# Linear attention in a two-layer trunk: chunk decays behind the first levels, sample operands of 128 rows, one product for key and query

## The chip, the cores and the metric

The kernel runs on one core of one Trainium2 chip. The metric is device time in microseconds for one launch. Five engines work side by side, each with its own queue of instructions that it takes in order: TensorE (PE, matrix products), VectorE (DVE), ScalarE (ACT, functions such as exp), GpSimd (POOL) and SyncE (SP, which issues transfers). An instruction that needs another engine's result waits on a semaphore, and all that stands behind it on its engine waits too.

## The reference, cut to what matters

Two layers, each with token mixing and a convolutional feed-forward part, over 64 sample tokens (8 sequences of 8) and 512 prompt tokens, model width 1024, all in f32. The mixing has softmax attention (8 heads), HGRN linear attention (4 heads, key 128, value 64) and GLA linear attention (4 heads, key 32, value 64). The change is in the last two, both of which compute:

```
def step(S, inp):                      # chunks of 64 tokens (8 for the samples)
    qc, kc, vc, gc = inp
    b = jnp.cumsum(gc, axis=2)         # summed log forget gates
    inter = einsum('nhtk,nhkv->nhtv', qc * jnp.exp(b), S)
    diff = b[:, :, :, None, :] - b[:, :, None, :, :]
    decay = where(causal, jnp.exp(jnp.minimum(diff, 0.0)), 0.0)
    scores = einsum('nhtk,nhsk,nhtsk->nhts', qc, kc, decay)
    intra = einsum('nhts,nhsv->nhtv', scores, vc)
    b_last = b[:, :, -1:, :]
    S = exp(b_last) * S + einsum('nhsk,nhsv->nhkv', kc * jnp.exp(b_last - b), vc)
    return S, inter + intra
```

## The kernel before

All 576 tokens are kept together, channels on partitions, in two halves of 320 and 256 tokens. An f32 projection is split into three products of rounded parts (lines 125, 126 and 127: weight-high by input-high, weight-low or input-low by the other's high part); one projection of 128 output channels is 24 such matmuls a half. Its weights come by DMA into `wraw`, ScalarE makes the high part `whi` (line 106), VectorE the low part `wlo` (line 107).

`mixing` goes through first projections, `values`, four HGRN heads (`hgrn_head`, j = 0 to 3), one tile with all four GLA heads (j = 4), then attention. Both kinds call `gla_tile`. It computes, with b the summed log gates:

- the diagonal: `own` = q x k (line 447), summed by small products (453, 455);
- six levels B = 1, 2, 4, 8, 16, 32 (`level_tile`): GpSimd takes differences of b within blocks (413, 414), ScalarE their exp (415), VectorE multiplies the early half by k (416) and the late half by q (418); TensorE multiplies the two (471 for the sample tokens, in the first three levels, 477 for the prompt), and VectorE copies the scores under a mask into `sds` and `sd` (439). The tile `lev` has two buffers;
- `qe` = exp(b) x q (483, 488), `al` (485, 486) and `ke` = exp(b_last - b) x k (499, 501, 502), the chunk decays;
- transposes of ke (508, 511), state products U for the prompt (517) and for the samples (531, with `vm` from GpSimd, 529), the running states;
- outputs from scores and states (548 to 557); line 554 is the samples' product of `vs` and `sds`.

`finish` normalises a pair of heads: `rsqrt` on GpSimd (243) gives `rh` and `rhs`, products at 692 to 706 spread them. The same helper gives `rr`, the norm of the inputs, which line 269 broadcasts before a layer's first decays. The sample operands have 64 rows (the 64 sample tokens), the prompt's 128.

The order in which each engine takes its instructions is not the order of the code: a scheduler in the framework simulates the engines and their dependences and moves independent work (projections of later heads above all) in between. Where the code says `with behind(ins)`, an instruction is not issued, in that simulation, before `ins`; the table FILL uses this to place some loads and projections.

```
def behind(ins):
    return tc.issue_after(ins) if ins is not None else nullcontext()
```

Of the kernel before, what the change touches and what calls it, by code (L numbers as in the profile page):

```python
# [8 lines left out]
F32 = mybir.dt.float32  # L9
# [4 lines left out]
ALU = mybir.AluOpType  # L14
# [5 lines left out]
P = 128  # L20
# [52 lines left out]
def trunk_kernel(ctx: ExitStack, tc: tile.TileContext, I, O):  # L73
# [329 lines left out]

    def level_tile(hp, q, k, b, B, t0, qbd):
# [6 lines left out]
        bv, ev, qv, kv = view(b), view(e), view(q), view(k)  # L411
        ref = bv[:, :, 0, B - 1:B].to_broadcast([P, n, B])
        G.tensor_tensor(ev[:, :, 0, :], ref, bv[:, :, 0, :], ALU.subtract)  # L413
        G.tensor_tensor(ev[:, :, 1, :], bv[:, :, 1, :], ref, ALU.subtract)
        S.activation(e[:, t0:T], e[:, t0:T], AF.Exp)
        V.tensor_tensor(ev[:, :, 0, :], ev[:, :, 0, :], kv[:, :, 0, :], ALU.mult)
        if qbd is None:
            V.tensor_tensor(ev[:, :, 1, :], ev[:, :, 1, :], qv[:, :, 1, :], ALU.mult)
        else:
            for h in range(4):  # L420
                r = slice(32 * h, 32 * h + 32)
                V.tensor_tensor(view(qbd[:, h, :])[r, :, 1, :], ev[r, :, 1, :], qv[r, :, 1, :], ALU.mult)
        return e

    def gla_tile(l, hp, q, k, b, heads, kd, vt, vs, vcol, s0, o_ps, os_ps, outs, qbd, j):

# [17 lines left out]
        sds = hp.tile([TS, nh, TS], F32, name="sds", tag=f"sds{nh}", bufs=2 if nh == 1 else 1)  # L444
        sdm = sd.rearrange("p c h t -> p (c h) t")
# [9 lines left out]
        PE.matmul(bp[:TS, 4 * nh:5 * nh], own[:, 0:TS], sums, start=True, stop=True)  # L455
        for dst, rows, c0 in ((sdm, P, 0), (sds, TS, 4 * nh)):
            m = dst.shape[1]
            V.tensor_tensor(dst, dmask[:rows, None, :].to_broadcast([rows, m, 64]),
                            bp[:rows, c0:c0 + m, None].to_broadcast([rows, m, 64]), ALU.mult)
        for lv, B in enumerate((1, 2, 4, 8, 16, 32)):  # L460
            sample = B <= 4
            xk = xq = level_tile(hp, q, k, b, B, 0 if sample else TS, qbd)
            if qbd is not None:
                xq = qbd

            def moving(c0):
                return late(xq[:, c0:c0 + 64] if qbd is None else xq[:, :, c0:c0 + 64], B)

            if sample:
                bs = s_bank()  # L470
                PE.matmul(bs[:TS, :nh * 32], xk[:, 0:TS], moving(0), start=True, stop=True)
                level_scores(B, lv, sds, bs[:TS, :nh * 32])
            bp = s_bank()
            for cp in range(4):
                for hh in range(2):
                    c0 = TS + P * cp + 64 * hh
                    mm = PE.matmul(bp[64 * hh:64 * hh + 64, cp * nh * 32:(cp + 1) * nh * 32],  # L477
                                   xk[:, c0:c0 + 64], moving(c0), start=True, stop=True)
            mark(f"h{j}.{lv}", mm)
            level_scores(B, lv, sdm, bp[:, :128 * nh])  # L480

        qe = hp.tile([P, T], F32, name="qe", tag="qe", bufs=2)
        S.activation(qe, b, AF.Exp)
        al = hp.tile([P, 16], F32, name="al", tag="al", bufs=2)
# [11 lines left out]
        for t0, t1, w in ((0, TS, 8), (TS, T, 64)):  # L496
            bv = b[:, t0:t1].rearrange("p (c t) -> p c t", t=w)
            n = (t1 - t0) // w
            G.tensor_tensor(ke[:, t0:t1].rearrange("p (c t) -> p c t", t=w),
                            bv[:, :, w - 1:w].to_broadcast([P, n, w]), bv, ALU.subtract)  # L500
        S.activation(ke, ke, AF.Exp)
        V.tensor_tensor(ke, ke, k, ALU.mult)

        kT = hp.tile([P, 512], F32, name="kT", tag="kT", bufs=1)
        kTs = hp.tile([TS, P], F32, name="kTs", tag="kTs", bufs=1)
        tb = t_bank()
# [4 lines left out]
        PE.transpose(tb[:TS, :P], ke[:, 0:TS], ident)  # L511
        S.activation(kTs, tb[:TS, :P], AF.Copy)

# [13 lines left out]
        for i, (r0, _, _) in enumerate(heads):  # L527
            vm = hp.tile([TS, NB, 64], F32, name="vm", tag="t512", bufs=2)
            G.tensor_tensor(vm, vs[:TS, None, vcol + i * 64:vcol + (i + 1) * 64].to_broadcast([TS, NB, 64]),
                            bmask[:, :, None].to_broadcast([TS, NB, 64]), ALU.mult)  # L530
            mm = PE.matmul(ub[r0:r0 + kd, :], kTs[:, r0:r0 + kd],
                           vm.rearrange("p b v -> p (b v)"), start=True, stop=True)
# [6 lines left out]
        def head_outputs(i):  # L539
# [5 lines left out]
            for c in range(8):  # L545
# [22 lines left out]
    def mixing(l, act, first):  # L568
# [16 lines left out]
        with ExitStack() as mx:  # L585
# [63 lines left out]
            with ExitStack() as hx:  # L649
                hp = hx.enter_context(tc.tile_pool(name=f"hp{l}", bufs=1, reuse_waits="tile"))  # L650
                vb = [hp.tile([P, 4, 2, 256], F32, name=f"vb{i}") for i in range(2)]
                for t in vb:
                    G.memset(t, 0.0)
                vbs = [hp.tile([P, 256], F32, name=f"vbs{i}") for i in range(2)]
                rt = hp.tile([P, 5, 16], F32, name="rt")
                wg = hp.tile([16, P], F32, name="wg")
                SP.dma_start(wg, I["w_g"][l])

                works = {}
# [58 lines left out]
                def hgrn_head(j):  # L718
# [6 lines left out]
                    V.tensor_tensor_scan(b, scm, f, 0.0, ALU.mult, ALU.add)  # L725
                    return gla_tile(l, hp, q, k, b, [(0, j % 2, j // 2)], P, vb[0], vbs[0], j * 64, s0,
                                    o_ps, os_ps, (O["hp"][l, j], O["hs"][l, j]), None, j)[0]

# [33 lines left out]
                for t0, n in HALVES:  # L762
# [8 lines left out]
                V.tensor_tensor_scan(b, scm, z, 0.0, ALU.mult, ALU.add)  # L771
                outputs = gla_tile(l, hp, q, k, b, [(32 * i, i % 2, 2 + i // 2) for i in range(4)], 32,
                                   vb[1], vbs[1], 0, s0, o_ps, os_ps, (O["gp"][l], O["gs"][l]), qbd, 4)
                for i in range(2):
# [518 lines left out]
```

## Time and profile before

| what | value |
|---|---|
| device time, median of 3 (lowest, highest) | 1745.67 us (1742.08, 1746.49) |
| the profiled execution's own time | 1746.23 us |
| its span in the profile | 1744.4 us |
| TensorE busy | 1685.0 us, 97% |
| VectorE, ScalarE, GpSimd busy | 63%, 43%, 26% |
| granted TensorE clock, mean over the span | 0.986 |

The linear-attention stage runs from about 37 to 262 us in layer 1 and from about 906 to 1130 us in layer 2. In the page and in the trace each instruction stands with its line of the kernel, its engine, and out<-in by the names of the tiles. Idle time in square brackets names what ended it.

### The profile page before, as it was taken

What the parts mean: (1) busy time and instruction counts of PE and PEld (TensorE: products, weight loads), DVE (VectorE), ACT (ScalarE), POOL (GpSimd) and SP (SyncE); (2) the same over time, 40 slices, a digit from 0 to 9 for tenths busy, and PEclk for the clock granted to TensorE, in tenths of its full rate; (3) what the DMA queues carried; (4) which work ended last, traced back from release to release, by engine and by line L of the source; (5) the groups of instructions that cost most, each with busy time, mean ns of one, the idle gap of its engine ahead of it and who ended that gap; (6) DMA issues with size and microseconds to landing.
All of it is one profiled execution on the core that took longest, in us unless ns stands there. A gap on an engine that the chain in (4) does not pass through costs nothing.

```text
span 1744.4 us, 36125 instructions
## 1 busy us (share of the span) xinstructions
PE 1685.0 (97%) x14688; PEld 1588.6 (91%) x14688; DVE 1100.8 (63%) x2220; ACT 747.3 (43%) x1289; POOL 450.8 (26%) x780
## 2 busy tenths in 40 slices
PE   8999999899999999999999999999999999999997
PEld 8888997689899999999998888967899999999997
DVE  6765665665874564666667666566577736647664
ACT  6644424464543332333356534254645333323331
POOL 4543432301610010110264543332044101001103
PEclk9999999999999999999999999999999999999999
DMA  5211236748253635632322212368463446266231
GB/s 180 75 62 57 82 114 238 274 176 300 86 185 115 241 107 190 236 129 88 117 85 87 68 51 89 133 251 316 136 256 136 144 168 217 78 226 254 72 108 55
DMA packets 65670, 260.93 MB, mean 150 GB/s; under 512 B 9664, under 2 KB 18144, under 8 KB 63968
## 3 DMA queue, kind: packets, MB, share of 16 engines
q1 hardware_dynamic: 65504, 258.62, 42.1%
q8 instruction: 116, 1.90, 0.4%
q14 instruction: 50, 0.41, 0.1%
HBM read 245.39 MB, written 80.31 MB: 187 GB/s over the span
## 4 chain that ended last, share of the span: by engine, by line
PE 85%; DVE 4%; ACT 4%; POOL 3%; issue 3%; DMA 1%; SPq 0%; POOLq 0%; ACTq 0%; DVEq 0%
PE ps_m L125 22%; PE ps_m L126 22%; PE ps_m L127 22%; PE ps_s L477 2%; PE ps_o L916 1%; PE ps_o L862 1%; PE ps_s L837 1%; POOL x L345 1%; PE ps_t L853 1%; DVE pi L849 1%; PE ps_m L397 1%; PE ps_m L396 1%; PE ps_m L398 1%; DMA wraw<-in_w_of 1%; PE ps_m L627 1%
## 5 line engine op out<-in xcount | busy, mean ns | idle before, releaser
L106 ACT ACTIVATE whi<-wraw 128x1024 fp32r<-128x1024 f32 (+4 forms) x232 | 222.2, 963 | 316.6 <-PE ps_m L126 230.1
L107 DVE TENSOR_TENSOR wlo<-wraw,whi 128x1024 fp32r<-128x1024 f32 (+4 forms) x232 | 261.2, 1130 | 139.2 <-ACT whi L106 132.9
L125 PE MATMUL ps_m<-xha,whi 128*128 128x320 f32 x1088 | 341.3, 314 | 0.7 <-DVE y L375 0.6
L126 PE MATMUL ps_m<-xla,whi 128*128 128x320 f32 x1088 | 340.1, 313 | 0.0
L127 PE MATMUL ps_m<-xha,wlo 128*128 128x320 f32 x1088 | 339.3, 313 | 0.0
L126 PE MATMUL ps_m<-xlb,whi 128*128 128x256 f32 x1088 | 310.9, 286 | 0.0
L127 PE MATMUL ps_m<-xhb,wlo 128*128 128x256 f32 x1088 | 310.6, 285 | 0.0
L125 PE MATMUL ps_m<-xhb,whi 128*128 128x256 f32 x1088 | 310.3, 285 | 0.2 <-DVE smx L894 0.2
L125 PEld LDWEIGHTS ps_m<-xhb,whi 128*128 128x128 f32 x1088 | 209.0, 192 | 3.9 <-issue 3.4
L127 PEld LDWEIGHTS ps_m<-xhb,wlo 128*128 128x128 f32 x1088 | 209.1, 192 | 1.3 <-issue 0.7
L126 PEld LDWEIGHTS ps_m<-xlb,whi 128*128 128x128 f32 x1088 | 208.9, 192 | 1.0 <-issue 0.2
L125 PEld LDWEIGHTS ps_m<-xha,whi 128*128 128x128 f32 x1088 | 206.9, 190 | 2.6 <-DVE y L375 1.1
L126 PEld LDWEIGHTS ps_m<-xla,whi 128*128 128x128 f32 x1088 | 206.6, 190 | 2.4 <-issue 1.7
L125 PE MATMUL ps_m<-hh,whi 128*128 128x320 f32 (+1 forms) x704 | 208.4, 296 | 0.2 <-DVE y L1061 0.2
L127 PE MATMUL ps_m<-hh,wlo 128*128 128x320 f32 (+1 forms) x704 | 208.3, 296 | 0.0
L126 PE MATMUL ps_m<-hl,whi 128*128 128x320 f32 (+1 forms) x704 | 208.0, 295 | 0.0
L127 PEld LDWEIGHTS ps_m<-xha,wlo 128*128 128x128 f32 x1088 | 205.9, 189 | 2.0 <-issue 1.5
L125 PEld LDWEIGHTS ps_m<-hh,whi 128*128 128x128 f32 x704 | 132.9, 189 | 0.4 <-DVE y L1061 0.4
L126 PEld LDWEIGHTS ps_m<-hl,whi 128*128 128x128 f32 x704 | 133.0, 189 | 0.0
L127 PEld LDWEIGHTS ps_m<-hh,wlo 128*128 128x128 f32 x704 | 132.8, 189 | 0.0
L1002 DVE TENSOR_TENSOR u<-ps_m,rbc 128x256 f32<-128x256 f32 x82 | 34.9, 425 | 115.9 <-PE ps_m L127 115.7
L413 POOL TENSOR_TENSOR lev<-work 128x288 f32<-128x288 f32 (+1 forms) x60 | 49.5, 825 | 157.9 <-DVE work L725 46.4
(305 smaller groups left out, 3254.3 us busy)
## 6 DMA issues: line engine op xcount, KB each, us to landing
wraw<-in_w_up SPq DMA_DIRECT2D x88, 512.0 KB, 3.7
kv<-in_ck SPq DMA_DIRECT2D x32, 768.0 KB, 6.8
kv<-in_cv SPq DMA_DIRECT2D x32, 768.0 KB, 6.7
out_ck<-in_ck SPq DMA_DIRECT2D x32, 768.0 KB, 7.4
out_cv<-in_cv SPq DMA_DIRECT2D x32, 768.0 KB, 6.5
wraw<-in_w_s SPq DMA_DIRECT2D x42, 512.0 KB, 3.5
wraw<-in_w_dn SPq DMA_DIRECT2D x32, 384.0 KB, 3.1
wraw<-in_w_v SPq DMA_DIRECT2D x12, 512.0 KB, 3.4
```

The source lines that it names most:

```text
L106: S.activation(hi[:, :n], raw[:, :n], AF.Copy)
L107: V.tensor_tensor(lo[:, :n], raw[:, :n], hi[:, :n].bitcast(F32), ALU.subtract)
L125: PE.matmul(out, ah, bh, start=(i == 0), stop=False)
L126: PE.matmul(out, ah, bl, start=False, stop=False)
L127: PE.matmul(out, al, bh, start=False, stop=(i == n - 1))
L345: (V if dram_out and k % 4 == 3 else G).tensor_tensor(xk, xk, yk, ALU.add)
L396: PE.matmul(b[:, :n], wh, xh, start=(k == 0), stop=False)
L397: PE.matmul(b[:, :n], wl, xh, start=False, stop=False)
L398: PE.matmul(b[:, :n], wh, xl, start=False, stop=(k == KT - 1))
L413: G.tensor_tensor(ev[:, :, 0, :], ref, bv[:, :, 0, :], ALU.subtract)
L477: mm = PE.matmul(bp[64 * hh:64 * hh + 64, cp * nh * 32:(cp + 1) * nh * 32], xk[:, c0:c0 + 64], moving(c0), start=True, stop=True)
L1002: V.tensor_tensor(u[:, 338:594], b[:, :n], R[:, t0:t0 + n], ALU.mult)
```

## The change

There are three parts. (1) In `gla_tile` the exp of qe is issued behind the second level's exp (`exps[1]`), the subtractions of ke behind the third level's second subtraction (`subs[2]`), and ke's exp behind the third level's exp. (2) `vbs`, `vm`, `sds` and `kTs` become tiles of 128 rows that live for a whole layer; eight GpSimd memsets at the layer's start put zeros into rows 64 to 127 (2048 columns in all), and the sample products at 531 and 554 contract over 128 rows. `vm` leaves the pair of buffers that it shared with `sn` and the squares of `finish`, and has two of its own. (3) For the HGRN heads one VectorE op multiplies the early half by k and the late half by q: the key takes the first slot of the tile `work` and the query the second, and a strided view reads both. The GLA tile keeps its separate products.

```
         G.tensor_tensor(ev[:, :, 0, :], ref, bv[:, :, 0, :], ALU.subtract)
-        G.tensor_tensor(ev[:, :, 1, :], bv[:, :, 1, :], ref, ALU.subtract)
-        S.activation(e[:, t0:T], e[:, t0:T], AF.Exp)
-        V.tensor_tensor(ev[:, :, 0, :], ev[:, :, 0, :], kv[:, :, 0, :], ALU.mult)
+        sub = G.tensor_tensor(ev[:, :, 1, :], bv[:, :, 1, :], ref, ALU.subtract)
+        exp = S.activation(e[:, t0:T], e[:, t0:T], AF.Exp)
         if qbd is None:
-            V.tensor_tensor(ev[:, :, 1, :], ev[:, :, 1, :], qv[:, :, 1, :], ALU.mult)
+            both = kq[:, t0:t0 + 2 * (T + B)].rearrange("p (two r) -> p two r", two=2)[:, :, 0:T - t0]
+            both = both.rearrange("p two (n x) -> p n two x", x=2 * B)[:, :, :, 0:B]
+            V.tensor_tensor(ev, ev, both, ALU.mult)
...
-        S.activation(qe, b, AF.Exp)
+        with behind(exps[1]):
+            S.activation(qe, b, AF.Exp)
...
-            G.tensor_tensor(ke[:, t0:t1].rearrange("p (c t) -> p c t", t=w),
-                            bv[:, :, w - 1:w].to_broadcast([P, n, w]), bv, ALU.subtract)
-        S.activation(ke, ke, AF.Exp)
+            with behind(subs[2]):
+                G.tensor_tensor(ke[:, t0:t1].rearrange("p (c t) -> p c t", t=w),
+                                bv[:, :, w - 1:w].to_broadcast([P, n, w]), bv, ALU.subtract)
+        with behind(exps[2]):
+            S.activation(ke, ke, AF.Exp)
...
-            vm = hp.tile([TS, NB, 64], F32, name="vm", tag="t512", bufs=2)
-            G.tensor_tensor(vm, vs[:TS, None, vcol + i * 64:vcol + (i + 1) * 64].to_broadcast([TS, NB, 64]),
+            vm = vms[(i + j) % 2]
+            G.tensor_tensor(vm[:TS], vs[:TS, None, vcol + i * 64:vcol + (i + 1) * 64].to_broadcast([TS, NB, 64]),
...
-            PE.matmul(os_[rows, :], vs[:TS, cols], sds[:, i, :], start=True, stop=False)
+            PE.matmul(os_[rows, :], vs[:, cols], sds[:, i, :], start=True, stop=False)
...
+                vms = [hp.tile([P, NB, 64], F32, name=f"vm{i}") for i in range(2)]
+                sds1 = [hp.tile([P, 1, TS], F32, name=f"sds{i}") for i in range(2)]
+                sds4 = hp.tile([P, 4, TS], F32, name="sds4")
+                kTs = hp.tile([P, P], F32, name="kTs")
+                for t in (*vbs, *vms, *sds1, sds4, kTs):
+                    G.memset(t[TS:], 0.0)
...
-                        works[j] = [t[:, i, :] for i in range(4)]
+                        kqs[j] = t.rearrange("p i t -> p (i t)")
+                        works[j] = [t[:, i, :] for i in (1, 0, 2, 3)]
```

The scheduler answers the new constraints with another order. On TensorE, head 0 of layer 1, the order was this, from the level-0 sample product (471) on; `ke` is the chunk decay of the keys, `xha` and the like are inputs of head 1's query projection:

```order
L471 MATMUL ps_s<-lev 64x32
L508 MATMUL ps_t<-con,ke 128x128 x4
L511 MATMUL ps_t<-con,ke 64x128
L125 MATMUL ps_m<-xha_141,whi 128x320
L126 MATMUL ps_m<-xla_143,whi 128x320
L125 MATMUL ps_m<-xhb_142,whi 128x256
L126 MATMUL ps_m<-xlb_144,whi 128x256
L477 MATMUL ps_s<-lev 64x32 x8
```

The transposes stood ahead of the projection. Now, at the same place (line 471 has become 480):

```order
L480 MATMUL ps_s<-lev 64x32
L125 MATMUL ps_m<-xha_141,whi 128x320
L126 MATMUL ps_m<-xla_143,whi 128x320
L125 MATMUL ps_m<-xhb_142,whi 128x256
L126 MATMUL ps_m<-xlb_144,whi 128x256
L127 MATMUL ps_m<-xha_141,wlo 128x320
L125 MATMUL ps_m<-xha_145,whi 128x320
```

The projection follows the sample product directly; the prompt's level-0 products come 30 projection matmuls later, the transposes after more than 70.

On ScalarE, same place, before (`vb` and `rt` are evacuations of `values`, `qe` belongs to heads 0 and 1):

```order
L483 ACT_TABLE_LOAD
L483 ACTIVATE qe_776<-work_314 128x576
L483 ACTIVATE qe_1006<-work_315 128x576
L415 ACTIVATE lev_671<-lev_671 128x576
L639 ACTIVATE rt_311<-ps_m_592,rr1_486 128x16
L645 ACTIVATE vb0_305<-ps_m_592,rr1_486 64x256 x2
L501 ACTIVATE ke_782<-ke_782 128x576
L106 ACTIVATE whi_823<-wraw_821 128x1024
```

and now:

```order
L417 ACT_TABLE_LOAD
L417 ACTIVATE lev_684<-lev_684 128x576
L650 ACTIVATE rt_325<-ps_m_606,rr1_500 128x16
L656 ACTIVATE vb0_305<-ps_m_606,rr1_500 64x256 x2
L106 ACTIVATE whi_828<-wraw_826 128x1024
L106 ACTIVATE whi_1049<-wraw_1047 128x1024
```

The level's exp comes first, and neither a qe nor a ke exp stands between it and the split of the weights.

On TensorE at the start of layer 2, the broadcast of `rr` (269) stood here among the first products of `values` (125 to 127 and 627):

```order
L127 MATMUL ps_m<-whi,xla_10040 128x272
L125 MATMUL ps_m<-whi,xha_10042 128x272
L269 MATMUL ps_t<-con,rr_10588 128x128 x2
L627 MATMUL ps_m<-wlo,xha_10042 128x272
L627 MATMUL ps_m<-whi,xha_10046 128x272
```

and now, 20 matmuls further on, here:

```order
L125 MATMUL ps_m<-whi,xha_10026 128x272
L126 MATMUL ps_m<-wlo,xha_10026 128x272
L269 MATMUL ps_t<-con,rr_10574 128x128 x2
L127 MATMUL ps_m<-whi,xla_10028 128x272
```

In layer 1 that broadcast has kept its place.

## Rows read from the trace of the kernel before

**Rows 1.** Page, part 1: each engine's busy us, share, instructions.

```profile
PE 1685.0 (97%) x14688; PEld 1588.6 (91%) x14688; DVE 1100.8 (63%) x2220; ACT 747.3 (43%) x1289; POOL 450.8 (26%) x780
```

**Rows 2.** Table by stretch: stretch and length, busy per engine, clock, DMA.

```profile
37.00:262.00 225.00, 216.83 (x2267) 198.11 (x2265) 150.20 (x290) 107.49 (x161) 95.79 (x110) 0.98 0.24 78
480.00:500.00 20.00, 20.00 (x153) 20.00 (x152) 15.84 (x27) 8.57 (x13) 4.62 (x14) 1.00 0.68 252
```

**Rows 3.** TensorE's waits: us in total, times, longest.

```profile
PE ps_s L471 <- DVE lev L418: 5.5, 2, 2.7
...
PE ps_t L508 <- DVE ke L502: 2.9, 2, 1.5
...
PE ps_s L453 <- DVE own L447: 2.5, 2, 1.3
...
PE ps_s L477 <- DVE lev L418: 2.0, 2, 1.0
...
PE ps_t L700 <- POOL rh L243: 1.4, 2, 0.7
```

**Rows 4.** Timeline, TensorE, head 0 of layer 1: start, us, instruction, wait.

```profile
49.72 0.27 PE L471 MATMUL ps_s<-lev 128*64 128x32 f32 x2 [2.72 <-DVE lev L418]
51.52 1.09 PE L508 MATMUL ps_t<-con,ke 128*128 128x128 f32 x4 [1.53 <-DVE ke L502]
...
52.48 0.62 PE L125 MATMUL ps_m<-xha,whi 128*128 128x320 f32 x1
```

**Rows 5.** Timeline, ScalarE, the same place.

```profile
45.77 1.26 ACT L483 ACTIVATE qe<-work 128x576 f32<-128x576 f32 x2
46.93 0.67 ACT L415 ACTIVATE lev<-lev 128x576 f32<-128x576 f32 x1
...
48.76 0.68 ACT L501 ACTIVATE ke<-ke 128x576 f32<-128x576 f32 x1
...
49.35 1.99 ACT L106 ACTIVATE whi<-wraw 128x1024 fp32r<-128x1024 f32 x2
```

**Rows 6.** Line 447, all instances: duration min/median/max in ns.

```profile
L447 DVE TENSOR_TENSOR own<-work x10: 743/754/1246, 39.6 to 1030.6; 128x576 f32<-128x576 f32 x10
```

**Rows 7.** Page, part 5: busy us, mean ns, idle before (line 107).

```profile
L107 DVE TENSOR_TENSOR wlo<-wraw,whi 128x1024 fp32r<-128x1024 f32 (+4 forms) x232 | 261.2, 1130 | 139.2 <-ACT whi L106 132.9
```

**Rows 8.** Timeline, GpSimd, start of layer 2.

```profile
896.76 3.55 POOL L653 MEMSET vb<- 128x2048 f32 x2
```

**Rows 9.** Timeline, GpSimd, start of layer 1.

```profile
32.02 1.41 POOL L243 TENSOR_TENSOR rr<-rv,mhalf 128x2 f32<-128x2 f32 x1 [1.77 <-DVE rv L242]
```

**Rows 10.** Table by stretch around the stretches of low clock.

```profile
52.00:58.00 6.00, 6.00 (x38) 5.68 (x37) 5.37 (x7) 3.56 (x7) 5.03 (x4) 0.55 0.52 178
922.00:926.00 4.00, 4.00 (x33) 3.71 (x33) 3.37 (x6) 2.71 (x5) 3.95 (x3) 0.70 0.61 200
142.00:147.00 5.00, 5.00 (x39) 4.48 (x39) 4.45 (x10) 1.44 (x3) 2.27 (x2) 0.66 0.29 94
```

**Rows 11.** Timeline, GpSimd, head 2 of layer 1.

```profile
112.66 1.29 POOL L499 TENSOR_TENSOR ke<-work 128x64 f32<-128x64 f32 x2
```

**Rows 12.** Timeline, three engines, head 2 of layer 1.

```profile
104.04 1.06 ACT L106 ACTIVATE whi<-wraw 128x1024 fp32r<-128x1024 f32 x1 [5.38 <-PE ps_m L126]
...
114.19 0.45 DVE L418 TENSOR_TENSOR lev<-lev,work 128x288 f32<-128x288 f32 x1
...
115.76 0.24 PE L471 MATMUL ps_s<-lev 128*64 128x32 f32 x1
```

**Rows 13.** Timeline, TensorE, state products of head 0.

```profile
60.08 1.05 PE L517 MATMUL ps_t<-vb,kT 128*128 128x128 f32 x8
61.06 1.12 PE L531 MATMUL ps_t<-vm,kTs 64*128 64x512 f32 x2
62.12 0.39 PE L125 MATMUL ps_m<-xhb,whi 128*128 128x256 f32 x1
```

**Rows 14.** Line 488, all instances.

```profile
L488 DVE TENSOR_TENSOR qe<-qe,work x8: 1215/1360/1584, 49.5 to 1006.7; 128x576 f32<-128x576 f32 x8
```

More of the change, by code (lines that the diff above doesn't have):

```diff
@@ L401, in first_tiles, with level_tile @@
                 e(b, hf, t0, n)
-    def level_tile(hp, q, k, b, B, t0, qbd):
+    def level_tile(hp, q, kq, b, B, t0, qbd):
         n = (T - t0) // (2 * B)
@@ L409, in view @@
             return t[:, t0:T].rearrange("p (n two w) -> p n two w", two=2, w=B)
-        bv, ev, qv, kv = view(b), view(e), view(q), view(k)
+        bv, ev = view(b), view(e)
         ref = bv[:, :, 0, B - 1:B].to_broadcast([P, n, B])
         G.tensor_tensor(ev[:, :, 0, :], ref, bv[:, :, 0, :], ALU.subtract)
-        G.tensor_tensor(ev[:, :, 1, :], bv[:, :, 1, :], ref, ALU.subtract)
-        S.activation(e[:, t0:T], e[:, t0:T], AF.Exp)
-        V.tensor_tensor(ev[:, :, 0, :], ev[:, :, 0, :], kv[:, :, 0, :], ALU.mult)
+        sub = G.tensor_tensor(ev[:, :, 1, :], bv[:, :, 1, :], ref, ALU.subtract)
+        exp = S.activation(e[:, t0:T], e[:, t0:T], AF.Exp)
         if qbd is None:
-            V.tensor_tensor(ev[:, :, 1, :], ev[:, :, 1, :], qv[:, :, 1, :], ALU.mult)
-        else:
+            both = kq[:, t0:t0 + 2 * (T + B)].rearrange("p (two r) -> p two r", two=2)[:, :, 0:T - t0]
+            both = both.rearrange("p two (n x) -> p n two x", x=2 * B)[:, :, :, 0:B]
+            V.tensor_tensor(ev, ev, both, ALU.mult)
+        else:
+            kv, qv = view(kq[:, 0:T]), view(q)
+            V.tensor_tensor(ev[:, :, 0, :], ev[:, :, 0, :], kv[:, :, 0, :], ALU.mult)
             for h in range(4):
@@ L422, in level_tile, with gla_tile @@
                 V.tensor_tensor(view(qbd[:, h, :])[r, :, 1, :], ev[r, :, 1, :], qv[r, :, 1, :], ALU.mult)
-        return e
-    def gla_tile(l, hp, q, k, b, heads, kd, vt, vs, vcol, s0, o_ps, os_ps, outs, qbd, j):
+        return e, sub.ins, exp.ins
+    def gla_tile(l, hp, kq, q, k, b, heads, kd, vt, vs, vcol, s0, o_ps, os_ps, outs, qbd, j, sds, vms, kTs):
         nh = len(heads)
@@ L443, in gla_tile @@
         sd = hp.tile([P, 4, nh, 64], F32, name="sd", tag=f"sd{nh}", bufs=2 if nh == 1 else 1)
-        sds = hp.tile([TS, nh, TS], F32, name="sds", tag=f"sds{nh}", bufs=2 if nh == 1 else 1)
         sdm = sd.rearrange("p c h t -> p (c h) t")
@@ L455, in gla_tile @@
         PE.matmul(bp[:TS, 4 * nh:5 * nh], own[:, 0:TS], sums, start=True, stop=True)
-        for dst, rows, c0 in ((sdm, P, 0), (sds, TS, 4 * nh)):
+        for dst, rows, c0 in ((sdm, P, 0), (sds[:TS], TS, 4 * nh)):
             m = dst.shape[1]
@@ L459, in gla_tile @@
                             bp[:rows, c0:c0 + m, None].to_broadcast([rows, m, 64]), ALU.mult)
+        subs, exps = [], []
         for lv, B in enumerate((1, 2, 4, 8, 16, 32)):
             sample = B <= 4
-            xk = xq = level_tile(hp, q, k, b, B, 0 if sample else TS, qbd)
+            xk, sub, exp = level_tile(hp, q, kq, b, B, 0 if sample else TS, qbd)
+            xq = xk
+            subs.append(sub)
+            exps.append(exp)
             if qbd is not None:
@@ L471, in gla_tile @@
                 PE.matmul(bs[:TS, :nh * 32], xk[:, 0:TS], moving(0), start=True, stop=True)
-                level_scores(B, lv, sds, bs[:TS, :nh * 32])
+                level_scores(B, lv, sds[:TS], bs[:TS, :nh * 32])
             bp = s_bank()
@@ L498, in gla_tile @@
             n = (t1 - t0) // w
-            G.tensor_tensor(ke[:, t0:t1].rearrange("p (c t) -> p c t", t=w),
-                            bv[:, :, w - 1:w].to_broadcast([P, n, w]), bv, ALU.subtract)
-        S.activation(ke, ke, AF.Exp)
+            with behind(subs[2]):
[3 more added lines that the diff above has]
+            S.activation(ke, ke, AF.Exp)
         V.tensor_tensor(ke, ke, k, ALU.mult)
         kT = hp.tile([P, 512], F32, name="kT", tag="kT", bufs=1)
-        kTs = hp.tile([TS, P], F32, name="kTs", tag="kTs", bufs=1)
         tb = t_bank()
@@ L511, in gla_tile @@
         PE.transpose(tb[:TS, :P], ke[:, 0:TS], ident)
-        S.activation(kTs, tb[:TS, :P], AF.Copy)
+        S.activation(kTs[:TS, :], tb[:TS, :P], AF.Copy)
         ub = t_bank()
@@ L657, in mixing @@
                 SP.dma_start(wg, I["w_g"][l])
-                works = {}
+                works, kqs = {}, {}
                 def work(j):
@@ L725, in hgrn_head @@
                     V.tensor_tensor_scan(b, scm, f, 0.0, ALU.mult, ALU.add)
-                    return gla_tile(l, hp, q, k, b, [(0, j % 2, j // 2)], P, vb[0], vbs[0], j * 64, s0,
-                                    o_ps, os_ps, (O["hp"][l, j], O["hs"][l, j]), None, j)[0]
+                    return gla_tile(l, hp, kqs[j], q, k, b, [(0, j % 2, j // 2)], P, vb[0], vbs[0], j * 64, s0,
+                                    o_ps, os_ps, (O["hp"][l, j], O["hs"][l, j]), None, j, sds1[j % 2], vms, kTs)[0]
                 outputs = []
@@ L771, in mixing @@
                 V.tensor_tensor_scan(b, scm, z, 0.0, ALU.mult, ALU.add)
-                outputs = gla_tile(l, hp, q, k, b, [(32 * i, i % 2, 2 + i // 2) for i in range(4)], 32,
-                                   vb[1], vbs[1], 0, s0, o_ps, os_ps, (O["gp"][l], O["gs"][l]), qbd, 4)
+                outputs = gla_tile(l, hp, kqs[4], q, k, b, [(32 * i, i % 2, 2 + i // 2) for i in range(4)], 32,
+                                   vb[1], vbs[1], 0, s0, o_ps, os_ps, (O["gp"][l], O["gs"][l]), qbd, 4,
+                                   sds4, vms, kTs)
                 for i in range(2):
```

## The prediction

> **What bounds the kernel now.** I read the page's busy line first: TensorE is busy 97% of a span of 1744.4 us, the next engine 63% [rows 1]. So what counts is the time in which TensorE waits, runs at its low clock, or streams something slower than need be. Then the table by stretch: the linear-attention stage of layer 1, 225 us, holds 216.83 us of TensorE work, that is 8.2 us of idling, where 20 us in the middle of the feed-forward part have none [rows 2]. The same table gives the pitch of a projection matmul, 20.00 / 153 = 0.131 us. The waits of TensorE say what those 8.2 us are: level products that wait for the decayed operands (5.5 us in two waits, one in each layer), transposes that wait for ke (2.9), the diagonal sums that wait for `own` (2.5), later level products (2.0), the norm's broadcast that waits for `rh` (1.4) [rows 3]. Every entry is there twice, one wait in each layer. All of these lie on the path, for TensorE has nothing else in front of it then, by its order.
>
> The biggest of them is one place, head 0 (the first linear-attention head). The level-0 sample product starts at 49.72 after 2.72 us of idling, the four transposes of ke at 51.52 after another 1.53, and only at 52.48 the first matmul of head 1's query projection [rows 4]. ScalarE's rows say why: two qe exps stand ahead of the level-0 exp (45.77 for 1.26 us, then 46.93), and the ke exp stands ahead of the weight split (48.76, then whi from 49.35) [rows 5]. So the work that TensorE needs last (transposes, state) is queued ahead of what it needs first.
>
> **Part by part.** *The exps moved.* On ScalarE the level-0 exp takes the place of the qe exps: it runs from 45.77 to 46.44. The product with the key and the query is then one VectorE op; the same shape of op, `own`, takes 0.75 us in the middle [rows 6], so the level-0 sample product can go at 47.3 instead of 49.72. Behind the exp stand the evacuations that filled 47.60 to 48.76 before, 1.16 us [rows 5], then head 1's weight split directly: whi from 47.6 to 48.6 (two took 1.99), and wlo on VectorE, 1.13 us on average [rows 7], until about 49.75. By the new order four projection matmuls need only whi (4 x 0.131 = 0.52 us, done in the gap), the rest follow without a stop. So the projection runs as though it had begun at 49.75 - 0.52 = 49.2. The transposes, which took from 51.52 to 52.48, are now 0.96 us of work further on, and some 0.2 us of small products move with them: 50.4 against 52.48, a gain of 2.1 us. What is late next is wlo, which then leaves about half of the 4.25 us of idling. Bounds: 0 (the fused op and the split both queue behind contended VectorE work) to 4.25.
>
> In layer 2 the same two waits stand (2.7 and 1.4 in the sums of [rows 3]), but something is put ahead: the eight zero fills come before the rsqrt `rr` on GpSimd. Together they have 2048 columns, as one fill of vb, which takes 3.55 / 2 = 1.8 us [rows 8]; that row ends where `rr` began, so `rr` is 1.8 us later, and the order puts its broadcast 20 matmuls later, 20 x 0.131 = 2.6 us. The decays start that much later and would give the gain back, but in layer 2 the new order also puts the whole of head 1's query projection ahead of the level-0 product, and its weights do not wait for `rr`. I take layer 1's 2.1 us here too; bounds are 0 and the whole 4.1, and -2.6 if the projection's split too hangs behind the late evacuations. In layer 1 the fills cost nothing: GpSimd stood idle 1.77 us ahead of `rr` [rows 9], as long as the fills take; without that cover it would be 1.8.
>
> *The clock.* After head 0's gap the granted clock is 0.55 over 52 to 58 us, with TensorE busy all of the 6.00, which costs 0.45 x 6 = 2.7 us; in layer 2 it is 0.70 over 922 to 926, 0.30 x 4 = 1.2 us [rows 10]. That is the lower of the two levels (1.2 GHz) for a part of the time, behind idling of 2.7 and 1.5 us with a few tiny products between. With idling of half the size and a projection in the middle of it I let half go: 3.9 / 2 = 1.95 us. Bounds 0 to 3.9. A second such stretch in layer 1, 142 to 147 at 0.66, costs 0.34 x 5 = 1.7 us [rows 10]; the change spreads the products there among projections differently, and I take half again, 0.85, with bounds -1.7 (it comes up in layer 2 as well) and 1.7.
>
> *The other heads.* Per layer they wait 1.25 for `own`, 1.0 for a level, 0.7 for `rh` [rows 3]. For `rh`: GpSimd ran the two ke subtractions, 1.29 us, ahead of vm and rh [rows 11]; with these behind level 2, rh comes 1.29 us earlier and the 0.7 go. The 1.0 goes too, since qe's and ke's VectorE ops leave from ahead of the level ops. `own` is not touched. Against it a new wait of 0.9 us is to be expected at head 2's level 0: from the weight split at 104.04, which starts when a TensorE projection (head 2's forget gate) has freed its buffers, TensorE needed until 115.76 for that head's level-0 product, 11.7 us, while VectorE was done at 114.64 (114.19 + 0.45), 1.1 us ahead [rows 12]. The new order has 35 projection matmuls in this stretch where 58 stood, 23 x 0.131 = 3.0 us less cover, and 26 small products moved in, at most 1.2 us: 1.8 to 3.0 less against 1.1 of slack, so 0.7 to 1.9; I take 0.9, because rh's own products move behind it. Net 2 x (1.0 + 0.7 - 0.9) = 1.6 us. Bounds -2.4 and 5.9.
>
> *The zero rows.* Eight U products of 128 contraction rows take 61.06 - 60.08 = 0.98 us for 1024 columns; the pair with 64 rows that follows has as many columns and lasts to 62.12, 1.06 us, and the matmul behind it shows 0.39 [rows 13]. With 128 rows I give the pair 0.98, and 0.04 for the weight load behind it, 0.12 us for each of eight HGRN heads: 1.0. Bounds 0 (the delay is the weight load's alone, and stays) and 2.0 (the four-head tile gains too). A loss is excluded by the 128-row products themselves, which are no slower a column.
>
> *Key and query in one op.* Two ops of half the columns take 0.45 us each where nothing disturbs them [rows 12]; one takes 0.75 as `own` does, or 1.22 to 1.58 as the qe product, the same shape, does in its eight instances [rows 14]. So a level gains 0.15 us or loses 0.3 to 0.7. VectorE is not the bound, so it counts only where TensorE waits for a level, five or six times: -4 to +1; I take 0, since head 0's term already has the 0.75. The Trainium skill, "SBUF — State Buffer", section "SBUF: two separate sides", holds that a VectorE op with two operands in SBUF and a GpSimd op that reads SBUF exclude each other for a whole instruction. The spread of the two rows, 0.743 to 1.246 and 1.215 to 1.584, agrees with it, and by it the fused op, which keeps the lock in one piece, would meet GpSimd's subtractions of the next level and cost the upper figure.
>
> **The sum.** 2.1 + 2.1 + 1.95 + 0.85 + 1.6 + 1.0 = 9.6 us. The profiled execution took 1746.23 us; 1746.2 - 9.6 = 1736.6. The median of the runs is 0.56 below the profiled one, so the forecast is 1736 us.
>
> **Rivals.**
> - *Slower.* The chain of head 2 keeps its pace of 10.6 us (104.04 to 114.64) and its fused op takes 1.4 instead of 0.9 beside GpSimd, while TensorE gets there 1.8 to 3.0 earlier. If head 3 and the first broadcast run dry in the same way, each layer has two such waits of about 1.9, and the clock falls behind them as it does behind head 0, 1.2 to 2.7 a layer [rows 10]: 2 x (3.8 + 2.0) = 11.6 lost against 2.1 + 2.1 + 1.0 gained and nothing of the other terms. That is 6.4 slower, 1752. It decides from about 2.6 us of new waiting a layer. For it: 58 became 35. Against it: level 0 no longer waits behind qe and ke there.
> - *No change.* Layer 2's 2.6 us of delay cancels its 2.1, and the clock still falls, since the gap is shorter but not gone; what remains is 2.1 + 1.0 + a little: 3 us, 1743. For it: the gaps in front of both slow stretches stay at about 2 us.
> - *Larger gain.* Neither slow stretch comes back (3.9 + 1.7 instead of 2.8), and the waits of the middle heads go for the most part (4.5 instead of 1.6): 9.6 + 2.8 + 2.9 = 15.3, 1730.
> - *The fills do nothing for TensorE*, the pair keeps its 1.06: 1.0 less, 1737, inside the forecast.
>
> **Chances and range.** The forecast's own case, some 1732 to 1740: 0.42. Larger gain: 0.15. No change to a small gain (1740 to 1747): 0.26. Slower: 0.17. I call within 0.3% (5.2 us of 1745.67, so 1740.4 to 1750.9) no change, which is about what a measurement of this kernel can tell. From the cases: faster 0.42 + 0.15 + 0.04 = 0.61; slower by more than that 0.11; the same 0.28. The range from 1727 to 1750 leaves out about one in ten on each side; the likeliest case alone has 1732 to 1740.
>
> **What would show it.** Right: TensorE's wait for the first level product in each layer falls to about a microsecond, no wait for ke is left in head 0, the projection of head 1 begins before 49 us, the wait for `rh` is gone; the 64-row pair's successor starts 0.1 us sooner; the clock over 52 to 58 is above 0.75. Wrong: a new wait of over 2 us for a level operand or `own` in heads 2 or 3, the clock as low as before, or the fused op at 1.2 us and more in its median with TensorE waiting behind it. In layer 2, a projection that begins only after 920 us would say that the fills cost their 2.6 us in full.

## The result: 1724.4 us, 1.2% faster, below the range

The changed kernel takes 1724.41 us in the median of four runs (1720.14 to 1725.66), the kernel before 1743.88 in the same comparison. The ratio is 0.988, with a 95% interval from 0.9859 to 0.9901: 17 to 25 us less, where 9.6 were forecast and 1727 was the lower end. The profiled execution took 1720.14 us, its span is 1718.4; that is 26.1 us below the one of the kernel before (1746.23), where the medians differ by 19.5, so 6.6 us of what the two profiles show is the choice of these two executions. The busy line that answers to [rows 1]:

```profile
PE 1668.6 (97%) x14688; PEld 1577.8 (92%) x14688; DVE 1089.8 (63%) x2172; ACT 747.4 (43%) x1290; POOL 462.6 (27%) x796
```

TensorE runs the same 14688 matmuls in 16.4 us less busy time, and idles 9.6 us less (1718.4 - 1668.6 = 49.8 against 59.4). To see where, the span is cut at the same pieces of work in both kernels: from head 0's diagonal sums to the last broadcast of the four-head tile (the linear-attention stage), and from there to the end of layer 1's mixing (its attention stage). The table by stretch, kernel before: layer 1's linear attention, layer 1's attention, layer 2's linear attention.

```profile
46.70:268.60 221.90, 213.73 (x2242) 194.71 (x2238) 146.14 (x285) 99.17 (x147) 93.67 (x108) 0.98 0.25 84
268.60:427.20 158.60, 147.68 (x1484) 120.90 (x1485) 94.53 (x285) 83.43 (x186) 29.74 (x28) 0.97 0.66 245
915.90:1135.30 219.40, 211.32 (x2239) 192.51 (x2236) 145.97 (x285) 99.15 (x147) 93.69 (x108) 0.98 0.25 85
```

The same three stretches of the changed kernel:

```profile
46.50:256.30 209.80, 205.83 (x2222) 189.14 (x2220) 141.32 (x261) 101.00 (x149) 97.11 (x108) 0.99 0.25 85
256.30:409.60 153.30, 146.04 (x1505) 119.62 (x1503) 95.16 (x286) 81.84 (x184) 30.04 (x28) 1.00 0.71 260
898.10:1112.00 213.90, 207.94 (x2239) 191.72 (x2237) 141.19 (x263) 101.23 (x149) 100.53 (x110) 0.99 0.25 84
```

The differences of the lengths are 12.1, 5.3 and 5.5 us, 22.9 of the 26.0 by which the two spans differ. Eighteen projection matmuls (2.4 us) went from the first stretch into the second, so like for like it is 9.7, 7.7 and 5.5. Adding up (1 - granted clock) x busy over stretches of 2 us gives what the low clock cost: 4.6, 4.8 and 2.1 us before, 1.5, 0 and 1.7 after. The other 3.1 us are short falls of the clock too, of 1.5 to 1.7 us each: outside these stretches the kernel before has four, the changed kernel two, and their number and place change from kernel to kernel.

Head 0, answering to [rows 4], on TensorE's timeline:

```profile
46.51 0.26 PE L460 MATMUL ps_s<-con,own 128*64 128x1 f32 x2
47.23 0.30 PE L480 MATMUL ps_s<-lev 128*64 128x32 f32 x2 [0.47 <-DVE lev L422]
48.50 0.57 PE L125 MATMUL ps_m<-xha,whi 128*128 128x320 f32 x1 [0.96 <-ACT whi L106]
...
49.76 0.64 PE L127 MATMUL ps_m<-xha,wlo 128*128 128x320 f32 x1
```

and on ScalarE's, answering to [rows 5]:

```profile
45.54 0.69 ACT L417 ACTIVATE lev<-lev 128x576 f32<-128x576 f32 x1
46.25 0.28 ACT L650 ACTIVATE rt<-ps_m,rr 128x16 f32<-128x16 f32 x1
46.42 0.94 ACT L656 ACTIVATE vb<-ps_m,rr 64x256 f32<-64x256 f32 x2
47.39 2.00 ACT L106 ACTIVATE whi<-wraw 128x1024 fp32r<-128x1024 f32 x2
```

The exp stands first, the split starts at 47.39, the first product with `wlo` runs at 49.76, where 49.75 was forecast (the diagonal sums ahead of it begin 0.2 us earlier than before, 46.51 against 46.74). The waits that answer to [rows 3], of the whole span:

```profile
PE ps_m L125 <- ACT whi L106: 2.6, 2, 1.6
...
PE ps_s L480 <- DVE lev L422: 1.8, 3, 1.1
...
PE ps_s L480 <- DVE sds L445: 1.5, 1, 1.5
PE ps_t L719 <- POOL rh L243: 1.4, 1, 1.4
PE ps_s L486 <- DVE lev L422: 1.1, 2, 0.9
...
PE ps_s L458 <- DVE own L452: 0.9, 1, 0.9
```

The wait for ke is gone, the one for `rh` is gone in layer 1 and doubled in layer 2.

### The profile page after: what moved, and what is told of

Read it like the earlier page. It is cut to its first block, busy times and chain, and to the rows that moved or that the text cites. A ratio compares the mean times of both kernels' runs of the same rounds, so it can differ in the third digit from the quotient of the medians.

```text
span 1718.4 us, 36060 instructions
## 1 busy us (share of the span) xinstructions
PE 1668.6 (97%) x14688; PEld 1577.8 (92%) x14688; DVE 1089.8 (63%) x2172; ACT 747.4 (43%) x1290; POOL 462.6 (27%) x796
## 4 chain that ended last, share of the span: by engine, by line
PE 86%; ACT 4%; DVE 3%; POOL 3%; issue 2%; DMA 1%; POOLq 0%; SPq 0%; ACTq 0%
PE ps_m L125 23%; PE ps_m L127 23%; PE ps_m L126 23%; PE ps_s L486 2%; PE ps_o L936 1%; PE ps_s L857 1%; PE ps_o L882 1%; POOL x L345 1%; PE ps_m L638 1%; PE ps_m L396 1%; PE ps_m L398 1%; PE ps_m L397 1%; PE ps_t L873 1%; DVE pi L869 1%; PE ps_t L528 1%
## 5 line engine op out<-in xcount | busy, mean ns | idle before, releaser
L1059 ACT ACTIVATE hh<-c 128x64 fp32r<-128x64 f32 x88 | 34.2, 435 | 120.3 <-DVE c L1048 120.3
```

Source lines behind the costliest of these rows:

```text
L1059: S.activation(dh, src, AF.Copy)
```

## The experiments

In all kernels below but e12 and e13 the slots of key and query in `work` are as in the change; that alone leaves TensorE's order as it was (e6, whose layer 1 has no other edit, runs the order of before up to head 0 of layer 2). Times are medians, beside the kernel before in the same comparison; a stage's length is from its profiled execution. Parts are numbered as in the change: (1) moves, (2) zero rows, (3) one product.

**The three parts alone, and the change without the first.** e1 is the kernel before with the two hunks of part (1), e2 with those of part (2), e3 with that of part (3), e4 has (2) and (3).

> The kernel before with the first part alone: qe, ke subtractions and ke exp queued behind the levels. Theory (waits and clock): TensorE's waits in both linear-attention stages fall by 4 to 6 us in all and the stretches of low clock there shrink by about 2.5 us, so 1743.9 becomes 1734 to 1738 (6 to 10 less). Rival (all the gain is from this part, the other two are nothing): 1724 to 1727. Rival of the prediction's sum: terms of the moves 2.1 + 2.1 + 2.0 + 0.9 + 1.6 = 8.6 less, 1735.

> The kernel before with the second part alone: 128-row sample operands with zero rows and the eight fills. Theory (every change of the matmul's row count costs TensorE about 0.1 to 0.2 us, both ways): in the traces the eight U products, the 64-row pair and the return to the projection last 0.36 us longer before than after, 8 heads give 2.9, the output products some 2 more: 4 to 5 less, 1739, unless layer 2's later rr takes 2.6 back. Rival of the prediction: 1.0 less, 1743, or slower by up to 1.6 with layer 2's fills.

> The kernel before with the third part alone: one VectorE op for key and query in the HGRN levels. Prediction: no change (within 1 us, 1743 to 1745), as VectorE is waited for in few places. Rival (the level's chain is shorter by one op's overhead, which tells at every level that TensorE waits for): 3 to 5 less, 1740. Rival (the longer op meets GpSimd's subtractions and takes 1.2 to 1.6 us): 2 to 4 more.

> The changed kernel without the first part (zero rows and the one product stay). If the parts add up: e2 plus e3, so 1739 by the theory of row changes. If the moves carry nearly all: 1742 to 1745.

The kernel before 1745.04. e1 1721.96, ratio 0.9872 (0.9851 to 0.9893); e2 1746.65, 1.0009 (0.9995 to 1.0023); e3 1753.68, 1.0047 (1.0024 to 1.0071); e4 1743.43, 1.0001 (0.9988 to 1.0014). The moves alone give all of the gain, over twice what the prediction had for them. e1 and e3 lie outside what was expected of them. The one product alone is slower, yet its own duration can't be why: TensorE's waits for the HGRN levels are 8.2 us in e3 against 7.5 in the kernel before, and the largest new wait is one of 4.05 us in each layer at the four-head tile, which keeps its separate products. How long the one product takes depends on its width. In the changed kernel (mean ns behind the busy us), first the levels that hold the sample tokens too, then the others:

```profile
L422 DVE TENSOR_TENSOR lev<-lev,work 128x576 f32<-128x576 f32 x24 | 25.1, 1045 | 14.5 <-ACT lev L417 14.5
L422 DVE TENSOR_TENSOR lev<-lev,work 128x512 f32<-128x512 f32 x24 | 18.0, 748 | 12.3 <-ACT lev L417 12.2
```

**One layer, and pairs of parts.** e5 and e6:

```
-        with behind(exps[1]):
+        with behind(exps[1] if l == 0 else None):   # e5; l == 1 in e6; so for subs[2] and exps[2]
```

e7 has (1) and (3), e8 has (1) and (2).

> The kernel before with the first part in layer 1 alone. The attention stage of layer 1 then has the new order of its projections, as with the moves in both layers. Theory (the moves gain twice: waits and low clock in the linear-attention stage, about 7 to 8 us a layer, and another 8 to 10 us because the scheduler orders layer 1's attention differently behind them): 16 to 18 less than before, 1727 to 1729. Rival (all of the gain is in the linear-attention stages, half in each): 11 to 12 less, 1733.

> The kernel before with the first part in layer 2 alone; layer 1's attention keeps the order of before. Theory (as above): 5 to 8 less, 1737 to 1740. Rival (half in each layer): 11 to 12 less, 1733.

> The changed kernel without the zero rows: moves and the one product. By its order, layer 1's attention has the projections where the kernel before has them. Theory (that order costs 8 to 10 us): 1722 of the moves alone plus 8 to 10 plus or minus the product's own part, so 1728 to 1734, and the profile shows about 10 us of idling and one or two stretches of low clock in layer 1's attention, as before. Rival (the attention's order is nothing, the stage differs by chance between executions): 1720 to 1725.

> The changed kernel without the one product: moves and zero rows. Theory of row changes (zero rows save TensorE about 4 us of busy time that the profiles of the changed kernel and of the moves alone differ by): 1718 to 1720, better than either. Rival (zero rows are worth nothing on the path, as alone): 1722 to 1725. Rival (the fills delay layer 2's decays by 2.6 us): 1724 to 1727.

The kernel before 1744.21. e5 1728.57, e6 1740.03, e7 1731.07, e8 1723.05. Layer 1's moves give 15.6 us, layer 2's 4.2. e5 to e7 come out as their theories said, to a tenth, e8 as its first rival. With the one product added to the moves (e7), 9.1 us are lost again. Its linear attention in layer 1 is as short as e1's, 213.8 us against 214.9; what differs is layer 1's attention. The table by stretch, that stage alone, first e7, then e1:

```profile
260.30:418.50 158.20, 148.86 (x1488) 121.59 (x1486) 94.30 (x285) 83.56 (x186) 29.71 (x28) 0.96 0.66 246
```

```profile
261.40:409.60 148.20, 142.86 (x1486) 116.54 (x1486) 91.71 (x285) 81.82 (x184) 30.45 (x28) 1.00 0.71 261
```

The part has the same work in both. In e7 the scheduler has placed its projections as in the kernel before (in the third pair of heads 18 and 6 stand where e1 has 19 and 5, and so on): 4 us more of idling (158.20 - 148.86 = 9.3 against 5.3), and a clock of 0.96. With that old order the stage takes 158 us (before, e6, e7), with nearly that order 156 (e2, e4); in all other kernels run it takes 148 to 154, e12 among them, whose order is the old one from the third pair on and another ahead of it.

**Late fills, the two halves of the moves, the gap filled.** e9 is e8 with the fills behind `rr`; e10 moves qe alone, e11 ke alone; e12 is the kernel before with idle work in the gap:

```
+                with behind(last_r[0].ins):          # e9: the pow that made rr
+                    for t in (*vbs, *vms, *sds1, sds4, kTs):
+                        G.memset(t[TS:], 0.0)
...
+        for _ in range(6 if j == 0 else 0):          # e12, behind the diagonal sums
+            PE.matmul(bp[:, 64:384], own[:, 0:128], own[:, 0:320], start=True, stop=True)
```

> Moves and zero rows (as e8), with the eight fills issued behind the rsqrt rr in each layer, so that layer 2's broadcast does not wait for them. Theory (the zero rows save TensorE 2 us and more a layer in matmul shape changes, and lose about 2.9 us again in layer 2, where e8 idles 6.7 us against 3.8 of the moves alone): 2 to 3 less than e8, 1720 to 1721, and layer 2's linear-attention stage at 212 to 213 us with under 4.5 us of idling. Rival (the fills cost nothing): as e8, 1722 to 1724.

> The kernel before with qe's exp alone behind the second level. By its order layer 1's attention has most of the new order of projections. Theory (attention order 8 to 10; of the linear-attention stages' 11 us only the level-0 wait's part, 1.3 us of ScalarE time a layer): 1730 to 1734. Rival (qe is the whole of the first wait and brings its clock too): 1724 to 1727.

> The kernel before with ke's subtractions and exp alone behind the third level. Layer 1's attention has the order of the changed kernel. Theory (the transposes leave from ahead of head 1's projection, so the projection fills the gap): 1724 to 1728. Rival (ke matters little, since its wait of 1.5 us is only half of the first): 1730 to 1734.

> The kernel before with six idle matmuls (128x320 f32, their output in columns that nobody reads) behind the diagonal sums of head 0 in each layer, where TensorE waits 2.7 us for level 0. Nothing of the chain of operands is changed. Theory (the clock falls behind that gap because TensorE idles there): the granted clock over the 6 us after the gap goes from 0.55 to above 0.85 in layer 1 and the stage gets 1.5 to 3 us shorter a layer, 1739 to 1742, if the attention keeps its time. Rival (the clock falls for another reason): clock as before and 1745 or later.

The kernel before 1744.23. e9 1730.26, e10 1755.03, e11 1739.73, e12 1766.15: no theory foresaw the times of e9, e10 or e11, and e12 has the time of its rival with the clock of its theory. The two halves of the moves, 10.8 us slower and 4.5 faster, do not add up to 23. But e12 answers its own question. Its table by stretch over the filled gap and the 6 us behind it:

```profile
47.00:52.00 5.00, 5.00 (x40) 3.62 (x38) 3.53 (x5) 4.94 (x9) 2.91 (x7) 1.00 0.00 0
52.00:58.00 6.00, 5.14 (x47) 4.63 (x46) 5.49 (x9) 4.35 (x9) 5.74 (x5) 1.00 0.59 190
```

and the gap in the kernel before:

```profile
47.00:52.00 5.00, 0.75 (x5) 0.70 (x6) 4.37 (x7) 4.90 (x11) 3.10 (x7) 0.86 0.00 0
```

With TensorE busy through the gap the clock stays at 1.00 (2.4 GHz), where the 6 us behind it had 0.55 [rows 10]: the idling brings the low level, not the work after it. The state product of head 0 comes at 58.75 instead of 61.06 [rows 13]. The loss is elsewhere, and most of it goes with another order: the linear-attention stages take 228.5 and 228.4 us, and the four-head tile waits 6.1 us for its level operands in each.

**The order disturbed by one matmul.** e13 is the kernel before, e14 is e1, each with one idle matmul of 64 columns for each layer. e15 makes the moves for head 0 alone, e16 for the others.

```
+        for _ in range(1 if j == 0 else 0):
+            PE.matmul(bp[:, 64:128], own[:, 0:128], own[:, 0:64], start=True, stop=True)
...
+        with behind(exps[1] if j == 0 else None):    # e15; j > 0 in e16
```

> The kernel before with one idle matmul of 64 columns behind head 0's diagonal sums in each layer; no exp, subtraction or tile is moved. It takes the scheduler to another order (416 lines of difference on TensorE), and layer 1's attention gets the order that the changed kernel and the moves have. Theory (the attention stage's part of the gain is that order and not the moves themselves): layer 1's attention stage at 148 to 152 us instead of 158.6, and the kernel at 1733 to 1738, where the linear-attention stages don't suffer. Rival (the moves cause the attention's gain by operands that come earlier): the stage at 156 to 159, 1744 to 1746.

> The moves alone (e1) with one idle matmul of 64 columns behind head 0's diagonal sums in each layer: 844 lines of difference in TensorE's order. Theory (the order behind the change is a matter of chance, worth several us either way): off e1's 1722 by over 3 us, more likely slower, 1725 to 1735. Rival (the moves make the kernel robustly faster): 1720 to 1724.

> The first part for head 0 of each layer alone; the other heads as before. Layer 1's attention has most of the new order. Theory (in the linear-attention stages the gain is mainly head 0's: its 4.1 us of waits and the low clock behind them): linear-attention stages at 215 to 217 us each, attention near 150, 1726 to 1731. Rival (the other heads carry it): stages at 219 to 222.

> The first part for heads 1 to 3 and the GLA tile, head 0 as before. Theory (head 0 carries the linear-attention gain): those stages at 219 to 221 us with head 0's waits of 2.7 and 1.5 us and its low clock still there, attention near 152, 1735 to 1738. Rival (the other heads carry it): stages at 215 to 217, 1727 to 1731.

The kernel before 1746.75. e13 1741.96 (ratio 0.9973, 0.9956 to 0.999), e14 1748.07 (1.0003), e15 1743.48, e16 1749.82. One idle matmul takes e1's whole gain away (e1 was 23.1 us below the kernel before beside it, e14 is 1.3 above), and it gives the kernel before the short attention stage without a single move. The table by stretch of e13, linear attention and attention of layer 1:

```profile
46.50:274.10 227.60, 215.04 (x2243) 196.32 (x2239) 144.10 (x285) 100.94 (x149) 91.45 (x108) 0.97 0.25 82
274.10:423.70 149.60, 144.29 (x1488) 116.95 (x1484) 93.55 (x284) 81.83 (x184) 30.15 (x28) 1.00 0.71 259
```

So the attention's 7 to 10 us belong to the order. Layer 2 shows the same: its attention has the same work, and in the kernel before it has the new order already (19 and 5) and takes 150.5 us. So only layer 1's stage had this to gain. In e10 layer 2 falls into the old order (18 and 6), while layer 1 gets the new one (149.1). Layer 2's attention, first the kernel before, then e10:

```profile
1135.30:1285.80 150.50, 145.08 (x1485) 117.92 (x1485) 94.56 (x285) 81.50 (x184) 30.16 (x28) 0.99 0.71 259
```

```profile
1136.30:1294.00 157.70, 149.20 (x1485) 121.88 (x1485) 93.61 (x285) 83.46 (x186) 29.80 (x28) 0.96 0.66 246
```

Of the 40 attention stages of all kernels, the 32 with 19 and 5 take 148 to 155 us; the eight with 18 and 6 take 156 to 159, but for e12's 153 in layer 1. e13's linear attention is 5.7 us longer than before in layer 1, though layer 2's is not (219.4). On its timeline the four-head tile's last level in layer 1:

```profile
239.69 1.97 PE L479 MATMUL ps_s<-work,lev 128*64 128x128 f32 x16 [3.68 <-DVE work L422]
```

By its order ten projections stand ahead of this product in layer 1; in layer 2 twenty-eight, as in the kernel before, and no such wait. e3, e10 and e15 have ten in both layers (e12 eleven), and their linear attention takes 222 to 229 us; e2 and e4 have them in layer 1, with 227 and 225. In every one of these places TensorE waits 3.7 to 4.3 us. e11, e14 and e16 have another order there, and so has e9 in layer 2 (the transposes six projections ahead of a level). The waits of e14 in that place:

```profile
PE ps_s L489 <- DVE work L428: 2.8, 1, 2.8
PE ps_s L483 <- DVE work L428: 2.3, 2, 1.8
```

None of these waits stands in e1, the changed kernel or the kernel before. e14's own forecast (1725 to 1735) was too low, e13's attention stage came as expected and its time did not, since its linear attention suffered, and e15 and e16 don't settle how the linear attention's gain divides between the heads, for both fell into one of these orders.

What the moves do at head 0 itself holds in every order. In layer 1 TensorE's gaps there come to 1.0 to 1.9 us in the ten kernels that move both for head 0, e14 and e15 among them, and to 3.9 to 5.7 us in the six that move neither (e12 left out); the low clock behind them lasts half as long. e15, which answers to [rows 4]:

```profile
47.49 0.27 PE L481 MATMUL ps_s<-lev 128*64 128x32 f32 x2 [0.46 <-DVE lev L422]
48.75 0.64 PE L125 MATMUL ps_m<-xha,whi 128*128 128x320 f32 x1 [0.98 <-ACT whi L106]
```

**Two kernels chosen by their order.** e17 is the change with late fills (as e9), e18 the change with the idle matmul (as e13).

> The changed kernel with its eight fills issued behind the rsqrt rr in each layer. Its order has 37 projections ahead of the four-head tile's last level products in both layers, as the changed kernel has in layer 1, and layer 1's attention as the changed kernel's. Theory (the order of the projections among the last levels decides, and the fills' delay of 2.6 us in layer 2 goes): 1720 to 1723, level with or better than the 1724 of the change. Rival (any other order loses, as e9 and e14 did): 1728 to 1750.

> The changed kernel with one idle matmul of 64 columns behind head 0's diagonal sums in each layer, the disturbance that e14 has. Its order has 38 projections between the four-head tile's last two full levels and 20 ahead of the last in both layers, as the moves alone (e1), and layer 1's attention as e1. Theory (the place of the projections in the order decides, not the disturbance): no loss, 1718 to 1725. Rival (the idle matmul itself or any disturbance costs the gain): 1735 to 1750, as e14.

The kernel before 1743.44. e17 1723.86, ratio 0.9877 (0.9854 to 0.99); e18 1721.62, 0.9868 (0.984 to 0.9896). Both came out as their order said: the same idle matmul that cost e14 its gain costs nothing where 38 projections are left ahead of the last level. Neither beats the change beyond the intervals, nor does e1.

## Why the prediction was wrong

The direction and the local mechanism were right; the sum failed. The step that failed is the part-by-part sum itself: it priced the moved instructions where the profile of before shows waits, 9.6 us, and gave no term to a stage whose code the change does not touch, though it compared the new order with the old in the linear attention. 7.7 us of layer 1's attention were missing, nearly half of the 16.4 by which the two profiled executions differ more than forecast; e7, e13 and e10's layer 2 tie them to the order of the projections there. The two linear-attention stages gave 15.2 us (6.3 of idling, 3.4 of low clock, 5.5 of other busy time) instead of 9.6; the mis-sized term there is the zero rows, 1.0 against the 5.5 (in e1, which has none, that part is 0.6). That the direction came out right was in part luck: e14, with the same moves, is no faster than the kernel before. By its terms:

- *The exps moved* (2.1 and 2.1). In layer 1 the time of the first `wlo` product was met, but the stage had begun 0.2 us earlier, so the gain is about 1.9. In layer 2 the projection follows with `wlo` at 901.25, 3.1 us behind the diagonal sums at 898.12; `rr` was 2.2 us late behind the fills (886.28, where vb's memsets end at 884.07; 1.8 was taken), and the projection covered it, as forecast.

```profile
880.52 3.55 POOL L664 MEMSET vb<- 128x2048 f32 x2
...
886.28 0.71 POOL L243 TENSOR_TENSOR rr<-rv,mhalf 128x2 f32<-128x2 f32 x1
```

- *The other heads* (1.6). The wait expected at head 2's level 0 came, 1.10 us against 0.9, in layer 1 only; `own`'s wait stayed in one layer of two, `rh`'s went in layer 1 and rose to 1.4 in layer 2. Together with head 0, idling in the two stages fell by 4.2 and 2.1 us, 6.3 against 5.8.
- *The clock* (1.95 + 0.85 = 2.8). In these stages 6.6 us of loss became 3.2, so 3.4: 1.7 at head 0 of the two layers and 1.7 from the second stretch, which did not come back. The prediction's window in layer 2, 922 to 926, caught 1.2 us of a fall that costs 2.1 from 918 on. Behind head 0 of layer 1 a fall is left, shorter:

```profile
48.00:54.00 6.00, 5.50 (x26) 5.21 (x27) 4.95 (x8) 4.70 (x8) 1.51 (x4) 0.72 0.49 145
```

  0.28 x 5.50 = 1.5 us instead of 2.7. e12 shows that the low clock goes when that gap is filled. What was not seen is that the attention stage's 4.8 us of low clock hang on idling too, and go with it.
- *The zero rows* (1.0). The rows that answer to [rows 13]:

```profile
68.46 1.05 PE L528 MATMUL ps_t<-vb,kT 128*128 128x128 f32 x8
69.35 1.02 PE L542 MATMUL ps_t<-vm,kTs 128*128 128x512 f32 x2
69.81 0.71 PE L127 MATMUL ps_m<-xha,wlo 128*128 128x320 f32 x1
70.36 0.31 PE L125 MATMUL ps_m<-xha,whi 128*128 128x320 f32 x1
```

  From the first U product to the second projection matmul it is 1.90 us. In the kernel before, the second projection matmul was

```profile
62.34 0.28 PE L126 MATMUL ps_m<-xlb,whi 128*128 128x256 f32 x1
```

  and so 62.34 - 60.08 = 2.26: 0.36 us a head, three times the 0.12 that was taken; if all eight heads are alike, 2.9. The whole passage with the 64-row pair in it is longer, not only the matmul behind it. The other 2.6 of the busy time (64-row output products, fewer changes of shape) were not taken apart. The Trainium skill, "TensorEngine Tiling (Array Packing)", section "Key Properties", says that changing the tiling mode drains TensorE. These rows fit that, if the 64-row pair runs in another mode, which no row shows. The prediction read only the pair and the matmul behind it. Yet e2 and e8 show no gain in time from it (1746.65 against 1745.04, 1723.05 against e1's 1721.96). e2 fell into the order with ten projections. In e8's layer 1 the linear attention is 2.1 us shorter than e1's at the same idling; in layer 2 TensorE idles 6.7 us where it idles 4.4 in e1, and what it saved is idled away.
- *The one product* (0). Level 0 of head 0 took 0.92 us where 0.75 was taken. Of the 24 products with 576 columns 16 took over 0.9 us, 1.7 at the most, and 15 of these ran beside a GpSimd op; in the level that holds the sample tokens being held up is the rule. By the exclusive lock of the Trainium skill, "SBUF — State Buffer", section "SBUF: two separate sides", such an op waits for a GpSimd op that began first. These rows agree in part: some products beside a GpSimd op took no longer (0.69 us with 512 columns). The two products of e8 that it replaces take 0.70 and 0.52 us in the mean with 288 columns each, so it is no longer than the pair. Its large effects are the order's: 8.1 us of new waits at the four-head tile in e3, layer 1's attention in e7.
- *Rivals.* The slower one (a chain that runs dry at heads 2 and 3) happened at its place with 1.1 us, and not beyond. But its kind is what the experiments are full of: the same moves with another order of projections (e14) lose all, not at head 2, but for the most part at the four-head tile's levels (10.3 us of waits in both layers, 7.6 of low clock, where e1 has none). The range had no room for either side of that.

What stays open: which single constraint turns the scheduler to the one or the other order; and the share of heads 1 to 3 in the linear attention's gain, since no run changed them alone and kept the order.

## What to carry to other kernels

Where a scheduler writes the order, an edit has two effects: what it does at its place, which the trace prices well, and a new draw of the order everywhere behind it, here worth up to 24 us. Before pricing, compare the new order stage by stage, also where no line has changed, and count the filler matmuls in front of each operand that is waited for; to know what an edit is worth, disturb the order by something idle and time it again. A gap on TensorE can cost its length and then the low clock behind it: head 0's 4.25 us of idling in layer 1 were followed by 2.7 us lost to the clock (52 to 58), so a wait that goes may give back more than its length.

## What the runs showed of the hardware

- Five us with 0.75 us of TensorE work (47 to 52 in the kernel before) were followed by 6 us at a mean clock of 0.55, a loss of 2.7 us; filled with matmuls whose result nobody reads, by 1.00.
- A pair of 64-row matmuls among 128-row ones costs 0.36 us, its way in and out together, though it has no more columns (2.26 against 1.90 us).
- A VectorE product of 128x576 f32, both operands in SBUF, took 0.74 us at the least; 16 of 24 took 0.9 to 1.7 us, 15 of them beside a GpSimd op.
